# Neighbours' taps of the convolution on ScalarE, and part of the weights' remainders by ScalarE and an accumulating transfer

## The chip, the cores and the metric

The kernel runs on one core of one Trainium2 chip. The metric is the device time of one execution in microseconds, the median of the runs shown. TensorE (PE) does the matrix products, VectorE (DVE), ScalarE (ACT) and GpSimd (POOL) work on tiles in SBUF and PSUM, and SyncE (SP) issues the loads.

## The reference

Two layers of an encoder on 256 tokens of width 2048, all in float32. Each layer normalises its input, projects it, runs two attention groups, projects back, and then does a gated feed-forward with a width-3 convolution over the positions. The change touches the feed-forward:

```python
def depthwise_conv(u, w, bias):
    up = jnp.pad(u, ((0, 0), (1, 1), (0, 0)))
    return up[:, :-2] * w[0] + up[:, 1:-1] * w[1] + up[:, 2:] * w[2] + bias
...
    for l in range(DEPTH):
...
        x = x + o @ w_out[l]
        h2 = rms_norm(x, ln2_g[l])
        u = depthwise_conv(h2 @ w_up[l], conv_w[l], conv_b[l])
        gate, up = u[..., :D_FF], u[..., D_FF:]
        x = x + (jax.nn.silu(gate) * up) @ w_down[l]
```

`w_up` is 2048 x 11264 and `w_down` 5632 x 2048 in each layer.

## The kernel before

**Products in parts.** A float32 product is made of products of fp32r operands. Each operand is split (`split`, lines 109 to 117) into a high part, which ACT rounds (L112), and a remainder, which DVE subtracts (L113). The tile names are `whi` and `wlo` for weights; an activation keeps both parts in one tile (`xs` for the normalised input, `mid` for the gated middle).

**Weights by the megabyte.** All weights come in quanta of 128 x 2048 float32 (1 MB), in the fixed order of the list `quanta`. SP loads each into one of three `raw` buffers (L741); the load of quantum q + 3 is issued when the last piece of quantum q has been split. A quantum is used in two half blocks of 128 x 1024 (three pieces for the seven products). The list `steps` holds these half blocks. `split_w(s + 4)` makes `whi` and `wlo` of the step that lies four ahead, then the step s itself is issued. There are five buffers of each, so a buffer is written again once PE has done with the step that used it five before.

**The up projection.** The 44 feature blocks f of a layer take two quanta each, u = 0 and 1, so four half blocks. In each half block PE does eight pairs (`two`): the high weights by both parts of `xs`, 512 wide, and the remainder of the weights by the high part of `xs`, 256 wide. The sums stand in a PSUM tile `mm`. After the fourth half block `glu(l, f)` follows: ACT copies the sum (L545), DVE adds the second half and scales by the norm into a `halo` tile (L546, L547), POOL copies its two edges (L549, L550), ACT does the centre tap with the bias (L555), DVE adds the four neighbour taps (two neighbours, gate and up; L557), ACT does SiLU (L559), DVE multiplies (L561), and the product is split into `mid`. Every second f forms four sums and differences for the seven products (`sums_mid`, L574 to L577).

**The down projection.** The 44 f of a layer are taken in chunks of 8, 8, 8, 8 and 12. After the ups of a chunk and one more f comes `q_plain` (a plain product of 128 rows, whose sum DVE adds to `x` at L654) and then four `q_seven`: two-by-two blocks by seven products, whose sums stand in PSUM tiles `mm`, `S`, `tr` and `pv`. Between the sevens lie quanta of `w_down` in the 8-wide chunks, and ups in the 12-wide one. The three pieces of a seven quantum need sums of weights, which DVE makes in place in `raw` before the second piece (`split_seven`, L747 to L749); the third piece is made of these too.

**Order.** A scheduler puts the instructions on the engines by their place in the program and by priority; the work of `split_w` has a priority of 40 (`AHEAD_PRIO`) ahead of its place. Each engine then runs its own list in order. Nothing in the scheduler is touched by the change. DMA loads go out on SP's queue; POOL issues none.

**The start.** The loop over `SPLIT_AHEAD` at line 836 makes the first four half blocks, each behind `first_x(i)`, which splits two blocks of `xs` (L115, L116). The first of them is split in two halves of 512 columns.

Of the kernel before, what the change touches and what calls it, by code (L numbers as in the profile page):

```python
# [11 lines left out]
F32 = mybir.dt.float32  # L12
# [6 lines left out]
P = 128  # L19
L = 2  # L20
T = 256
# [38 lines left out]
def encoder_kernel(  # L60
# [343 lines left out]

    quanta = []
    side = {}

    def at(q, f, *args, half=1):
        side.setdefault((q, half), []).append((f, args))

    def two(ps, w_h, w_l, mv, first, last):

        mm(ps, w_h, mv, first, False)
        mm(ps[:, 1], w_l, mv[:, 0], False, last)

# [111 lines left out]
    def q_up(l, f, u):  # L527
        def body(q, half, hi, lo):
            if u == 0 and half == 0:
                cur["up"] = psum.tile([P, 2, 2, T], F32, name="mm", bufs=2)  # L530
            ps = cur["up"]
            hv, lv = (w.rearrange("p (k j n) -> p k j n", k=4, j=2) for w in (hi, lo))
            for j in range(2):
                for kk in range(4):
                    k = 8 * u + 4 * half + kk
                    two(ps[:, j], hv[:, kk, j], lv[:, kk, j], xs[k], k == 0, k == KD - 1)
            if u == 1 and half == 1:
                glu(l, f, ps)
        return body

    def glu(l, f, ps):
# [8 lines left out]
        nc.gpsimd.tensor_copy(ux[:, :, T + r:T + 2 * r - 1], ux[:, :, r + 1:2 * r])  # L550
        y = work.tile([P, 2, T], F32, name="pT", bufs=4)
        for j in range(2):
            c = j * NF + f
            w0, w1, w2, b = (par["conv"][:, l, i, c:c + 1] for i in range(4))
            nc.scalar.activation(y[:, j, :], ux[:, j, r:r + T], AF.Identity, scale=w1, bias=b)  # L555
            for w, o in ((w0, 0), (w2, 2 * r)):
                nc.vector.scalar_tensor_tensor(y[:, j, :], ux[:, j, o:o + T], w, y[:, j, :],  # L557
                                               op0=ALU.mult, op1=ALU.add)
        nc.scalar.activation(t[:, 0, :], y[:, 0, :], AF.Silu)  # L559
# [139 lines left out]
    for l in range(L):  # L699
# [8 lines left out]
        for c, nf in enumerate(CHUNKS):  # L708
            up = lambda f: [(a["w_up"][l, f, u], q_up(l, f, u), "up") for u in range(2)]
            down = lambda nb, g: [(a["w_down"][l, sum(CHUNKS[:c]) // FG + g, nb], q_down(l, c, nb, g), "")]  # L710
# [7 lines left out]
            if nf == PART:  # L718
                for i in range(PAIRS):
                    quanta += seven(i) + down(2 + i // 2, i % 2)  # L720
            else:

                for i in range(PAIRS):
                    quanta += seven(i)
                    if f < NF:
                        quanta += up(f)
                        f += 1
                for nb, g in ((2, 0), (2, 1), (2, 2), (0, 2), (3, 0), (1, 2), (3, 1), (3, 2)):
                    quanta += down(nb, g)


    steps = [(q, h) for q in range(len(quanta)) for h in range(3 if quanta[q][2] == "seven" else 2)]
    raw, hl, left, loads, highs = {}, {}, {}, {}, {}

    def load(q, parts=1):
# [15 lines left out]

    def split_w(s, parts=1):
        if s < len(steps):
# [5 lines left out]
            with tc.high_priority(offset=AHEAD_PRIO if s >= KD // 2 else 0):  # L759
                if kind == "seven":  # L760
                    highs[s] = split_seven(raw[q].rearrange("p (k n) -> p k n", k=4), half, *hl[s])
                else:
                    m = 1024 // parts
                    for j in range(parts):
                        highs[s] = split(*(t[:, j * m:(j + 1) * m] for t in hl[s]),
                                         raw[q][:, half * 1024 + j * m:half * 1024 + (j + 1) * m])
            left[q] -= 1
# [68 lines left out]
    for i in range(SPLIT_AHEAD):  # L836
        first_x(i)
        split_w(i, 2 if i == 0 else 1)
    for n, shape, dt, src in (
# [121 lines left out]
```

## Time and profile before

| what | value |
|---|---|
| median of three runs | 2092.12 us (2092.11 to 2092.13) |
| the profiled execution, its own time | 2092.0 us |
| its span in the trace | 2090.2 us |
| granted TensorE clock | 1.000 |
| ACT busy | 1222.3 us (58%) |
| POOL busy | 170.3 us (8%) |
| moved | 408.42 MB, mean 195 GB/s |
| loads on SP's queue (q1) | 405.46 MB, 56.2% of the 16 DMA engines' span |

The profile is of one execution. Its span runs from the first to the last recorded instruction; 1.8 us of its own time lie outside. An engine's share is its busy time over the span, an average over stages with different limits. In a list of instructions the columns are start, length (both us), engine, line, operation, output and inputs, shape and count, and in brackets what ended the idle time before. A matmul's recorded length is not its spacing from the next: they are pipelined.

### The profile page before, as it was taken

The numbers are of one execution on the slowest core, as the hardware profiler recorded it, in microseconds if no ns is written. First come the engines' busy times: TensorE is split into PE (matmuls) and PEld (weight loads), VectorE is DVE, ScalarE is ACT, GpSimd is POOL, SyncE is SP. The second block draws the span as 40 slices with busy tenths as digits, with TensorE's granted clock in tenths as the row PEclk, the third lists the DMA queues.
The fourth block names the chain that finished last, engine by engine and source line by source line (L and its number), as shares of the span: only waits on it lengthen the run. The fifth ranks groups of instructions, "written<-read, shape, count | busy, mean of one in ns | idle before, by whom it ended". The sixth has DMA issues, their size and how long they took to land.

```text
span 2090.2 us, 29185 instructions
## 1 busy us (share of the span) xinstructions
PE 2083.5 (100%) x10816; PEld 1789.2 (86%) x10816; DVE 1720.5 (82%) x2604; ACT 1222.3 (58%) x1817; POOL 170.3 (8%) x237
## 2 busy tenths in 40 slices
PE   9999999999999999999999999999999999999999
PEld 8888888888888888888888888888888888888887
DVE  7786757898898988989757866678989989899896
ACT  7566556555555556556555665565556555555563
POOL 0011100100101001010000011001001010010100
PEclk9999999999999999999999999999999999999999
DMA  9544555556565564655655444555555655556554
GB/s 350 199 145 164 179 172 174 198 195 211 180 241 182 208 210 167 242 193 211 208 181 181 162 160 166 177 182 189 214 202 170 236 199 204 201 185 234 185 200 161
DMA packets 62144, 408.42 MB, mean 195 GB/s; under 512 B 7344, under 2 KB 9904, under 8 KB 13744
## 3 DMA queue, kind: packets, MB, share of 16 engines
q1 hardware_dynamic: 61280, 405.46, 56.2%
q8 instruction: 85, 1.39, 0.3%
q10 hardware_dynamic: 720, 1.08, 0.2%
q14 instruction: 59, 0.48, 0.1%
HBM read 404.42 MB, written 2.10 MB: 194 GB/s over the span
## 4 chain that ended last, share of the span: by engine, by line
PE 99%; DMA 0%; ACT 0%; DVE 0%; issue 0%
PE mm L98 90%; PE S L98 4%; PE pv L98 3%; PE tr L98 2%; PE tr L373 1%; PE tr L307 1%; PE S L149 1%; DMA head<-in_head 0%; ACT qtok L274 0%; ACT kT L315 0%; ACT xs L115 0%; DVE x L688 0%; ACT whi L112 0%
## 5 line engine op out<-in xcount | busy, mean ns | idle before, releaser
L112 ACT ACTIVATE whi<-raw 128x1024 fp32r<-128x1024 f32 (+1 forms) x797 | 830.9, 1057 | 689.9 <-PE mm L98 411.9
L113 DVE TENSOR_TENSOR wlo<-raw,whi 128x1024 fp32r<-128x1024 f32 (+1 forms) x797 | 963.9, 1220 | 270.3 <-ACT whi L112 231.8
L98 PE MATMUL mm<-xs,whi 128*128 128x512 f32 x2816 | 977.0, 390 | 0.0
L98 PE MATMUL mm<-xs,wlo 128*128 128x256 f32 x2816 | 794.1, 282 | 0.0
L98 PEld LDWEIGHTS mm<-xs,whi 128*128 128x128 f32 x2816 | 528.3, 188 | 110.5
L98 PEld LDWEIGHTS mm<-xs,wlo 128*128 128x128 f32 x2816 | 532.2, 189 | 1.1
L98 PE MATMUL mm<-whi,mid 128*128 128x512 f32 x1412 | 368.2, 391 | 0.0
L98 PEld LDWEIGHTS mm<-whi,mid 128*128 128x128 f32 x1412 | 263.0, 188 | 53.9
L98 PE MATMUL mm<-whi,xs 128*128 128x512 f32 x1152 | 294.2, 393 | 1.4 <-ACT qtok L274 1.3
L98 PEld LDWEIGHTS mm<-whi,xs 128*128 128x128 f32 x1152 | 213.1, 188 | 44.7 <-ACT qtok L274 1.8
L98 PE MATMUL mm<-wlo,mid 128*128 128x512 f32 x706 | 202.4, 392 | 0.0
L98 PE MATMUL mm<-wlo,xs 128*128 128x512 f32 x576 | 159.5, 393 | 0.0
L98 PEld LDWEIGHTS mm<-wlo,mid 128*128 128x128 f32 x706 | 132.1, 188 | 27.0
L557 DVE SCALAR_TENSOR_TENSOR pT<-halo,conv,pT 128x256 f32<-128x256 f32 x352 | 148.1, 478 | 0.9
L549 POOL COPY halo<-halo 128x6 f32<-128x6 f32 x88 | 39.6, 450 | 1232.6 <-DVE halo L547 1232.6
L98 PEld LDWEIGHTS mm<-wlo,xs 128*128 128x128 f32 x576 | 107.3, 188 | 21.6
L555 ACT ACTIVATE pT<-halo,conv 128x256 f32<-128x256 f32 x176 | 95.1, 587 | 5.8 <-DVE halo L547 5.7
L550 POOL COPY halo<-halo 128x6 f32<-128x6 f32 x88 | 77.1, 876 | 0.2 <-POOL halo L549 0.2
L547 DVE TENSOR_TENSOR halo<-prob,acc_b 128x512 f32<-128x512 f32 x88 | 60.6, 689 | 1.9
L546 DVE TENSOR_TENSOR prob<-prob,mm 128x512 f32<-128x512 f32 x88 | 59.8, 679 | 0.0
L545 ACT ACTIVATE prob<-mm 128x512 f32<-128x512 f32 x88 | 51.3, 583 | 7.1 <-PE mm L98 7.1
L559 ACT ACTIVATE prob<-pT 128x256 f32<-128x256 f32 x88 | 35.5, 404 | 30.0 <-DVE pT L557 30.0
(180 smaller groups left out, 1475.4 us busy)
## 6 DMA issues: line engine op xcount, KB each, us to landing
raw<-in_w_up SPq DMA_DIRECT2D x176, 1024.0 KB, 4.9
raw<-in_w_in SPq DMA_DIRECT2D x71, 1024.0 KB, 4.9
raw<-in_w_down SPq DMA_DIRECT2D x48, 1024.0 KB, 4.8
raw<-in_w_seven SPq DMA_DIRECT2D x40, 1024.0 KB, 4.9
raw<-in_w_out SPq DMA_DIRECT2D x32, 1024.0 KB, 4.9
raw<-in_w_plain SPq DMA_DIRECT2D x10, 1024.0 KB, 4.8
bias<-in_bias SPq DMA_DIRECT2D x16, 160.0 KB, 3.1
x<-in_x SPq DMA_DIRECT2D x4, 512.0 KB, 10.7
```

Of the source, the lines that this page charges most:

```text
L98: nc.tensor.matmul(ps, lhsT, rhs, start=start, stop=stop, skip_group_check=True)
L112: high = nc.scalar.activation(hi, src, AF.Copy)
L113: nc.vector.tensor_sub(lo, src, hi.bitcast(F32))
L149: nc.tensor.transpose(ps[:, j, tt * P:(tt + 1) * P], x[:, tt, (k + j) * P:(k + j + 1) * P], ident)
L545: nc.scalar.activation(t, ps[:, :, 0], AF.Copy)
L546: nc.vector.tensor_add(t, t, ps[:, :, 1])
L547: nc.vector.tensor_mul(ux[:, :, r:r + T], t, st["r2"][:, None, :].to_broadcast([P, 2, T]))
L549: nc.gpsimd.tensor_copy(ux[:, :, 1:r], ux[:, :, T:T + r - 1])
L550: nc.gpsimd.tensor_copy(ux[:, :, T + r:T + 2 * r - 1], ux[:, :, r + 1:2 * r])
L555: nc.scalar.activation(y[:, j, :], ux[:, j, r:r + T], AF.Identity, scale=w1, bias=b)
L557: nc.vector.scalar_tensor_tensor(y[:, j, :], ux[:, j, o:o + T], w, y[:, j, :], op0=ALU.mult, op1=ALU.add)
L559: nc.scalar.activation(t[:, 0, :], y[:, 0, :], AF.Silu)
```

## The change

It has four parts.

- **Taps.** In `glu`, the two taps of each neighbour (gate and up) are made by two ACT copies with a scale from the table into a tile `z`, and one DVE addition over both halves adds `z` to `y`. Before, DVE did the four taps by four multiply-add instructions. `y` and `z` share the four buffers of the name `pT`.
- **Remainders.** In the last half block of an f (u = 1, half = 1), unless one of the five steps before it belongs to a seven (`added`), DVE no longer subtracts the remainder. ACT writes the negated weights, rounded to fp32r, into `wlo`; POOL issues a transfer that adds the weights in DRAM to what stands in `wlo`; and ACT makes `whi` as before. The built program holds 82 of these half blocks, of 88 f.
- **Grouping.** In the last half block of every f, `two` takes all eight terms: first the eight products of the high weights, then the eight of the remainders. Elsewhere it goes pair by pair as before.
- **Start.** The first half block's high part is made by DVE, both halves before the first two blocks of `xs`, and its remainder behind them. `split_w` no longer takes a number of parts.

The order of the quanta, of SP's loads, and the number of buffers stay. The lists of `seven` and `down` quanta are appended one by one, so that `up` sees the length of `quanta`.

```diff
@@ -403,15 +403,19 @@
 
 
     quanta = []
+    second = set()
     side = {}
 
     def at(q, f, *args, half=1):
         side.setdefault((q, half), []).append((f, args))
 
-    def two(ps, w_h, w_l, mv, first, last):
-
-        mm(ps, w_h, mv, first, False)
-        mm(ps[:, 1], w_l, mv[:, 0], False, last)
+    def two(terms, late=False):
+
+        for group in [terms] if late else [[t] for t in terms]:
+            for ps, w_h, w_l, mv, first, last in group:
+                mm(ps, w_h, mv, first, False)
+            for ps, w_h, w_l, mv, first, last in group:
+                mm(ps[:, 1], w_l, mv[:, 0], False, last)
 
     def three(ps, terms, hv, lv, first, last, apart=False):
 
@@ -530,10 +534,8 @@
                 cur["up"] = psum.tile([P, 2, 2, T], F32, name="mm", bufs=2)
             ps = cur["up"]
             hv, lv = (w.rearrange("p (k j n) -> p k j n", k=4, j=2) for w in (hi, lo))
-            for j in range(2):
-                for kk in range(4):
-                    k = 8 * u + 4 * half + kk
-                    two(ps[:, j], hv[:, kk, j], lv[:, kk, j], xs[k], k == 0, k == KD - 1)
+            two([(ps[:, j], hv[:, kk, j], lv[:, kk, j], xs[k], k == 0, k == KD - 1)
+                 for j in range(2) for kk, k in enumerate(range(8 * u + 4 * half, 8 * u + 4 * half + 4))], u == half == 1)
             if u == 1 and half == 1:
                 glu(l, f, ps)
         return body
@@ -549,13 +551,15 @@
         nc.gpsimd.tensor_copy(ux[:, :, 1:r], ux[:, :, T:T + r - 1])
         nc.gpsimd.tensor_copy(ux[:, :, T + r:T + 2 * r - 1], ux[:, :, r + 1:2 * r])
         y = work.tile([P, 2, T], F32, name="pT", bufs=4)
+        w = [[par["conv"][:, l, i, j * NF + f:j * NF + f + 1] for i in range(4)] for j in range(2)]
         for j in range(2):
-            c = j * NF + f
-            w0, w1, w2, b = (par["conv"][:, l, i, c:c + 1] for i in range(4))
-            nc.scalar.activation(y[:, j, :], ux[:, j, r:r + T], AF.Identity, scale=w1, bias=b)
-            for w, o in ((w0, 0), (w2, 2 * r)):
-                nc.vector.scalar_tensor_tensor(y[:, j, :], ux[:, j, o:o + T], w, y[:, j, :],
-                                               op0=ALU.mult, op1=ALU.add)
+            nc.scalar.activation(y[:, j, :], ux[:, j, r:r + T], AF.Identity, scale=w[j][1], bias=w[j][3])
+
+        for i, o in ((0, 0), (2, 2 * r)):
+            z = work.tile([P, 2, T], F32, name="pT", bufs=4)
+            for j in range(2):
+                nc.scalar.activation(z[:, j, :], ux[:, j, o:o + T], AF.Copy, scale=w[j][i])
+            nc.vector.tensor_add(y, y, z)
         nc.scalar.activation(t[:, 0, :], y[:, 0, :], AF.Silu)
         m = work.tile([P, T], F32, name="bias", bufs=2)
         nc.vector.tensor_mul(m, t[:, 0, :], y[:, 1, :])
@@ -706,7 +710,10 @@
                     quanta.append((a["w_out"][l, 0 if grp == "a" else 1, nb, u], q_wout(l, grp, nb, u), ""))
         f = 0
         for c, nf in enumerate(CHUNKS):
-            up = lambda f: [(a["w_up"][l, f, u], q_up(l, f, u), "up") for u in range(2)]
+            def up(f):
+                second.add(len(quanta) + 1)
+                return [(a["w_up"][l, f, u], q_up(l, f, u), "up") for u in range(2)]
+
             down = lambda nb, g: [(a["w_down"][l, sum(CHUNKS[:c]) // FG + g, nb], q_down(l, c, nb, g), "")]
             seven = lambda i: [(a["w_seven"][l, c, i], q_seven(l, c, i), "seven")]
 
@@ -717,7 +724,8 @@
             quanta.append((a["w_plain"][l, c], q_plain(l, c), ""))
             if nf == PART:
                 for i in range(PAIRS):
-                    quanta += seven(i) + down(2 + i // 2, i % 2)
+                    quanta += seven(i)
+                    quanta += down(2 + i // 2, i % 2)
             else:
 
                 for i in range(PAIRS):
@@ -732,6 +740,12 @@
     steps = [(q, h) for q in range(len(quanta)) for h in range(3 if quanta[q][2] == "seven" else 2)]
     raw, hl, left, loads, highs = {}, {}, {}, {}, {}
 
+    def added(s):
+
+        q, half = steps[s]
+        return quanta[q][2] == "up" and quanta[q - 1][2] == "up" and half == 1 and q in second and \
+            not any(quanta[steps[i][0]][2] == "seven" for i in range(s - SPLIT_AHEAD - 1, s))
+
     def load(q, parts=1):
         if q < len(quanta):
             raw[q] = wp.tile([P, 2048], F32, name="raw", bufs=3)
@@ -749,7 +763,7 @@
             nc.vector.tensor_sub(w[:, 0], w[:, 3], w[:, 0])
         return split(hv, lv, (w[:, 1::2], w[:, 1:3], w[:, 0::3])[part])
 
-    def split_w(s, parts=1):
+    def split_w(s):
         if s < len(steps):
             q, half = steps[s]
             kind = quanta[q][2]
@@ -760,10 +774,24 @@
                 if kind == "seven":
                     highs[s] = split_seven(raw[q].rearrange("p (k n) -> p k n", k=4), half, *hl[s])
                 else:
-                    m = 1024 // parts
-                    for j in range(parts):
-                        highs[s] = split(*(t[:, j * m:(j + 1) * m] for t in hl[s]),
-                                         raw[q][:, half * 1024 + j * m:half * 1024 + (j + 1) * m])
+                    w = raw[q][:, half * 1024:(half + 1) * 1024]
+                    if s == 0:
+
+                        m = [slice(j * 512, (j + 1) * 512) for j in range(2)]
+                        for j in m:
+                            highs[s] = nc.vector.tensor_copy(hl[s][0][:, j], w[:, j])
+                        first_x(0)
+                        with tc.issue_after(highs[s].ins):
+                            for j in m:
+                                nc.vector.tensor_sub(hl[s][1][:, j], w[:, j], hl[s][0][:, j].bitcast(F32))
+                    elif added(s):
+
+                        nc.scalar.activation(hl[s][1], w, AF.Copy, scale=-1.0)
+                        nc.gpsimd.dma_start(out=hl[s][1], in_=quanta[q][0][:, half * 1024:(half + 1) * 1024],
+                                            accum_op=ALU.add)
+                        highs[s] = nc.scalar.activation(hl[s][0], w, AF.Copy)
+                    else:
+                        highs[s] = split(*hl[s], w)
             left[q] -= 1
             if left[q] == 0:
                 del raw[q]
@@ -834,8 +862,9 @@
         mm(ps[:, 0:P], ones, ones, True, True)
 
     for i in range(SPLIT_AHEAD):
-        first_x(i)
-        split_w(i, 2 if i == 0 else 1)
+        if i > 0:
+            first_x(i)
+        split_w(i)
     for n, shape, dt, src in (
             ("pos", [P, TT], I32, a["pos"]),
             ("inv", [P, HD // 2], F32, a["inv"].partition_broadcast(P))):
```

The rows below show how the issue order of three engines changes. They have the line, the operation, the output and the inputs, and the shape; "x2" stands for two such in a row. Lines after the change are those of the changed kernel (L545, L555, L557, L559, L654 and L747 to L749 become L547, L556, L561 with L562, L563, L658 and L761 to L763).

First ACT's list in one f of an up projection, from the copy of the sum (`prob<-mm`) to the split of the product (`mid<-bias`), before:

```order
L112 ACTIVATE whi<-raw 128x1024
L545 ACTIVATE prob<-mm 128x512
L112 ACTIVATE whi<-raw 128x1024
L555 ACTIVATE pT<-halo_110,conv 128x256 x2
L112 ACTIVATE whi<-raw 128x1024
L559 ACTIVATE prob<-pT 128x256
L112 ACTIVATE whi<-raw 128x1024
L112 ACTIVATE mid<-bias 128x256
```

The same stretch of ACT's list after the change:

```order
L547 ACTIVATE prob<-mm 128x512
L112 ACTIVATE whi<-raw 128x1024
L556 ACTIVATE pT<-halo_112,conv 128x256 x2
L561 ACTIVATE pT<-halo_112,conv 128x256 x4
L112 ACTIVATE whi<-raw 128x1024
L563 ACTIVATE prob<-pT 128x256
L792 ACTIVATE whi<-raw 128x1024
L789 ACTIVATE wlo<-raw 128x1024
L112 ACTIVATE mid<-bias 128x256
```

Four taps stand behind the centre taps (L556), and in one of the four half blocks the negated copy (L789) stands behind the high part (L792).

On POOL the transfer (L790) stands behind the two copies of the halo's edges (L551, L552) of the f before; before the change POOL's list had only the copies there.

Next DVE's list where the ups of an 8-wide chunk end and its sevens begin: from the sum of the plain product (`x<-x,mm`) to the last preparation of the second seven's weights (`raw<-raw`; `mid<-tq,mid` is the remainder of a sum made by `sums_mid`), before:

```order
L654 TENSOR_TENSOR x<-x,mm 128x512
L113 TENSOR_TENSOR wlo<-raw,whi 128x1024
L113 TENSOR_TENSOR mid<-tq,mid 128x256
L113 TENSOR_TENSOR wlo<-raw,whi 128x1024
L557 SCALAR_TENSOR_TENSOR pT<-halo_110,conv,pT 128x256 x2
L113 TENSOR_TENSOR wlo<-raw,whi 128x1024
L557 SCALAR_TENSOR_TENSOR pT<-halo_110,conv,pT 128x256 x2
L747 TENSOR_TENSOR raw<-raw 128x1024
L561 TENSOR_TENSOR bias<-prob,pT 128x256
L748 TENSOR_TENSOR raw<-raw 128x512
L749 TENSOR_TENSOR raw<-raw 128x512
```

The same place of DVE's list after the change:

```order
L658 TENSOR_TENSOR x<-x,mm 128x512
L549 TENSOR_TENSOR halo_110<-prob,acc_b 128x2x256
L113 TENSOR_TENSOR wlo<-raw,whi 128x1024 x2
L113 TENSOR_TENSOR mid<-tq,mid 128x256
L113 TENSOR_TENSOR wlo<-raw,whi 128x1024 x2
L562 TENSOR_TENSOR pT<-pT 128x512
L761 TENSOR_TENSOR raw<-raw 128x1024
L562 TENSOR_TENSOR pT<-pT 128x512
L762 TENSOR_TENSOR raw<-raw 128x512
L113 TENSOR_TENSOR wlo<-raw,whi 128x1024
L763 TENSOR_TENSOR raw<-raw 128x512
```

The sum of the plain product now stands ahead of the halo's product (L549), which stood ahead of it before, and a remainder of weights stands between the second and the third preparation.

Last PE's list at the same place, up to the third piece of the second seven (the two `pv<-whi,mid` at the end; `mm`, `tr`, `S` and `pv` are the PSUM tiles of the sums), before:

```order
L98 MATMUL mm<-whi,mid 128x512 x8
L98 MATMUL mm<-wlo,mid 128x512 x4
L98 MATMUL mm<-whi,mid 128x512 x8
L98 MATMUL tr<-whi,mid 128x512 x2
L98 MATMUL mm<-whi,mid 128x512 x2
L98 MATMUL mm<-wlo,mid 128x512 x4
L98 MATMUL tr<-wlo,mid 128x512
L98 MATMUL mm<-wlo,mid 128x512
L98 MATMUL S<-whi,mid 128x512 x4
L98 MATMUL pv<-whi,mid 128x512 x2
```

PE's list there after the change:

```order
L98 MATMUL pv<-wlo,mid 128x512
L98 MATMUL mm<-wlo,mid 128x512
L98 MATMUL tr<-whi,mid 128x512 x2
L98 MATMUL mm<-whi,mid 128x512 x2
L98 MATMUL mm<-wlo,mid 128x512 x4
L98 MATMUL mm<-whi,mid 128x512 x8
L98 MATMUL mm<-wlo,mid 128x512 x4
L98 MATMUL tr<-wlo,mid 128x512
L98 MATMUL mm<-wlo,mid 128x512
L98 MATMUL S<-whi,mid 128x512 x4
L98 MATMUL S<-wlo,mid 128x512 x2
L98 MATMUL pv<-whi,mid 128x512 x2
```

Two remainder products (`S<-wlo,mid`) now stand ahead of the third piece's first product: 51 products lie between the plain product's last one and that, 49 before.

## The prediction

> **What bounds the kernel now.** I read the page's head and its chain first, then busy time by stretch, then groups of instructions, then the timeline where the lead of the helpers is smallest.
>
> ```profile
> span 2090.2 us, 29185 instructions
> ...
> PE 2083.5 (100%) x10816; PEld 1789.2 (86%) x10816; DVE 1720.5 (82%) x2604; ACT 1222.3 (58%) x1817; POOL 170.3 (8%) x237
> ...
> PE 99%; DMA 0%; ACT 0%; DVE 0%; issue 0%
> ...
> 597.40:692.10 94.70, 94.70 (x540) 83.59 (x539) 83.02 (x128) 54.79 (x79) 8.39 (x14) 1.00 0.59 204
> 692.10:727.00 34.90, 34.90 (x155) 28.90 (x155) 34.59 (x40) 21.11 (x25) 1.18 (x2) 1.00 0.56 202
> ```
>
> The last two rows are a stretch of up projections and the stretch of seven-product down projections behind it (columns: PE, PEld, DVE, ACT, POOL, clock, DMA share and GB/s). The chain is PE for 99%, and PE has no gap in either stretch, at the full granted clock. DVE is at 88% in the ups (83.02 of 94.70) and at 99% in the sevens. So work taken from DVE in the ups can gain nothing by itself: PE does not wait for it. The question is only whether PE starts to wait somewhere. It can do so where the split weights arrive latest before their use, and that is early in each seven stretch. DVE and ACT enter it some 10 us ahead and use that lead up:
>
> ```profile
> 692.84 0.62 PE L98 MATMUL mm<-wlo,mid 128*128 128x512 f32 x2
> ...
> 704.40 0.62 PE L98 MATMUL pv<-whi,mid 128*128 128x512 f32 x2
> ...
> 703.05 3.91 ACT L112 ACTIVATE whi<-raw 128x1024 fp32r<-128x1024 f32 x4 [0.32 <-DVE raw L749]
> ...
> 692.39 0.68 DVE L547 TENSOR_TENSOR halo<-prob,acc_b 128x512 f32<-128x512 f32 x1
> ...
> 694.13 0.68 DVE L654 TENSOR_TENSOR x<-x,mm 128x512 f32<-128x512 f32 x1
> 694.73 1.22 DVE L113 TENSOR_TENSOR wlo<-raw,whi 128x1024 fp32r<-128x1024 f32 x1
> 695.86 0.42 DVE L113 TENSOR_TENSOR mid<-tq,mid 128x256 fp32r<-128x256 f32 x1
> ...
> 697.33 0.87 DVE L557 SCALAR_TENSOR_TENSOR pT<-halo,conv,pT 128x256 f32<-128x256 f32 x2
> ...
> 700.05 1.22 DVE L747 TENSOR_TENSOR raw<-raw 128x1024 f32<-128x1024 f32 x1
> 701.19 0.42 DVE L561 TENSOR_TENSOR bias<-prob,pT 128x256 f32<-128x256 f32 x1
> 701.53 0.68 DVE L748 TENSOR_TENSOR raw<-raw 128x512 f32<-128x512 f32 x1
> 702.24 0.69 DVE L749 TENSOR_TENSOR raw<-raw 128x512 f32<-128x512 f32 x1
> 702.85 1.22 DVE L113 TENSOR_TENSOR wlo<-raw,whi 128x1024 fp32r<-128x1024 f32 x1
> ```
>
> Columns: start, length, engine, line, tiles, count. The first PE row is the end of the plain product. The second uses the high part of the third piece of the second seven. ACT makes that piece as the first of the four at 703.05, when DVE's L749 ends (702.93): done at 703.05 + 1.06 = 704.11, used at 704.40. **The lead there is 0.3 us.** The other stretches between 8-wide chunks look the same, eight in all.
>
> **What the change removes and adds.**
>
> ```profile
> L112 ACT ACTIVATE whi<-raw 128x1024 fp32r<-128x1024 f32 (+1 forms) x797 | 830.9, 1057 | 689.9 <-PE mm L98 411.9
> ...
> L113 DVE TENSOR_TENSOR wlo<-raw,whi 128x1024 fp32r<-128x1024 f32 (+1 forms) x797 | 963.9, 1220 | 270.3 <-ACT whi L112 231.8
> ...
> L557 DVE SCALAR_TENSOR_TENSOR pT<-halo,conv,pT 128x256 f32<-128x256 f32 x352 | 148.1, 478 | 0.9
> ...
> L115 ACT ACTIVATE xs<-S,head 128x256 fp32r<-128x256 f32 x48 | 20.7, 469 | 12.0 <-PE S L149 8.8 <-DVE xs L116 3.2
> ```
>
> Taps: 352 DVE instructions of 478 ns go; 176 additions of 0.68 us (as L547 above) and 352 ACT instructions come, each near the 469 ns of L115, the nearest ACT row with one scale from a table. DVE gains 168 - 120 = 48 us, ACT gets 165. Remainders: the built program has 82 of them. DVE loses 82 x 1.22 = 100 us, ACT gets 82 x 1.06 = 87. All of it lies beside PE. In an up stretch of eight f, DVE falls to about 83.02 - 8 x 1.2 - 8 x 0.5 = 69 us of 94.70, and ACT rises to 54.79 + 8 x (1.0 + 4 x 0.47) = 78. Both keep up.
>
> The Trainium skill (ScalarE: Activation LUTs, Rules for kernel authors) says to put multiplications and additions on VectorE, not ScalarE. By it the taps would get dearer. The rows do not bear it out for these fp32 tiles (478 against 469 ns), so the sum stays as it is.
>
> Does ACT fit in detail? One f of an up stretch now:
>
> ```profile
> 400.39 1.06 ACT L112 ACTIVATE whi<-raw 128x1024 fp32r<-128x1024 f32 x1 [1.24 <-PE mm L98]
> 401.36 1.08 ACT L555 ACTIVATE pT<-halo,conv 128x256 f32<-128x256 f32 x2
> 403.15 1.06 ACT L112 ACTIVATE whi<-raw 128x1024 fp32r<-128x1024 f32 x1 [0.72 <-ACT pT L555]
> 405.93 1.06 ACT L112 ACTIVATE whi<-raw 128x1024 fp32r<-128x1024 f32 x1 [1.42 <-PE mm L98]
> 408.70 1.06 ACT L112 ACTIVATE whi<-raw 128x1024 fp32r<-128x1024 f32 x1 [0.78 <-ACT mid L112]
> ...
> 401.50 1.26 POOL L550 COPY halo<-halo 128x6 f32<-128x6 f32 x1
> ```
>
> PE frees a buffer every 2.77 us (405.93 to 408.70). After L555 ends at 402.44 come four taps, the last two not before POOL's copy ends (402.76): until about 404.5. The high part of 403.15 slips to 404.5, that of 405.93 stays, SiLU takes 0.4, and the negated copy runs 407.3 to 408.4, just before the buffer of 408.70. ACT fits.
>
> **The transfer.** PE takes up a block four half blocks after its buffer came free: 405.9 + 4 x 2.77 = 417.0. Eight wide products (0.227 us each, below) come first, so the remainder is wanted at 418.8, and 10.4 us remain after the copy. No row shows an accumulating transfer. Nearest are these:
>
> ```profile
> raw<-in_w_up SPq DMA_DIRECT2D x176, 1024.0 KB, 4.9
> ...
> x<-in_x SPq DMA_DIRECT2D x4, 512.0 KB, 10.7
> ```
>
> 4.9 us for twice the bytes, and 10.7 us for the same bytes in the crowded first 30 us. I take 5 to 9, near the first, because the ups leave the DMA engines 41% idle: no cost. At 10.7 it would be 0.3 us late 82 times, 25 us. Each further microsecond costs 82 us. Behind the waiting matmuls stands all of PE; behind the transfer on POOL stand only the next f's halo copies.
>
> The Trainium skill (DMA: Bandwidth & Descriptors, Anatomy of one DMA) gives 2.0 us plus bytes over 436 GB/s for a transfer issued by POOL, 3.2 us here as an estimate, and says nothing there of the addition. By it the transfer is hidden with 7 us to spare, as by the 4.9 us row.
>
> **Grouping.** In the last half block of an f eight 512-wide products now precede eight 256-wide ones.
>
> ```profile
> 399.55 0.39 PE L98 MATMUL mm<-xs,whi 128*128 128x512 f32 x1
> ...
> 399.90 0.39 PE L98 MATMUL mm<-xs,whi 128*128 128x512 f32 x1
> ...
> L98 PE MATMUL mm<-xs,wlo 128*128 128x256 f32 x2816 | 794.1, 282 | 0.0
> ...
> 172.07 0.85 PE L98 MATMUL pv<-pT,v_b 128*128 128x256 f32 x6
> ...
> 7.11 1.90 ACT L115 ACTIVATE xs<-mid,head 128x256 fp32r<-128x256 f32 x4
> 8.91 1.05 ACT L112 ACTIVATE whi<-raw 128x1024 fp32r<-128x1024 f32 x1
> ...
> 10.01 2.11 PE L98 MATMUL mm<-whi,xs 128*128 128x512 f32 x8
> ...
> 15.59 1.98 PE L98 MATMUL mm<-whi,xs 128*128 128x512 f32 x8
> ```
>
> An alternating pair takes 0.35 us. In runs of its own kind a 512 takes 0.227 (the last plain product starts at 692.84 + 0.62 - 0.39 = 693.07, and 50 products lie from there to 704.40) and a 256 takes (0.85 - 0.28) / 5 = 0.114 (six in 0.85, one lasts 0.28), 0.341 in all. The gain is 0 to 5 ns for each of 704 pairs; I take 1 ns, **-0.7 us**.
>
> **The start.** DVE now makes the first high part. But PE runs without gaps only from 10.01, when ACT has the next high part (8.91 + 1.05). Before it ACT makes four xs whose last source lands late. Bounds: 0, or the 1.0 us that ACT is spared. I take **-0.2**, near nothing.
>
> **The second seven, where I see the loss.** The issue order of DVE changes at that place. Before: sum of the plain product (L654), remainder, mid, remainder, two taps, remainder, two taps, L747, L561, L748, L749. After: sum, halo, two remainders, mid, two remainders, addition, first preparation, addition, second preparation, **a remainder, and only then the third preparation**. The order cannot start before the plain product is in: 693.07 + 0.39 = 693.46 (first PE row), so 693.55; before, DVE came to it late anyway, at 694.13. From there, start to start by the rows above: sum 0.60, halo 0.60, four remainders 4 x 1.13, mid 0.34, additions 2 x 0.60, preparations 1.14 and 0.60, and a remainder 1.14 with 0.1 of waiting for ACT. That is 10.2 us, so the third preparation starts at 703.8 and ends 0.69 later at 704.5. ACT follows 0.12 later (702.93 to 703.05) and takes 1.06: **705.65**. PE's own order puts two more products ahead of the piece, so it wants it at 704.40 + 2 x 0.227 = 704.85. It waits 0.8 us, 0.05 for the hand-over and 0.13 to get going (eight products take 2.11 us behind the wait that ends at 10.01, 1.98 at 15.59): **1.0 us, eight times, 8.0 us**. In the two wide chunks the same sum and halo come ahead of two remainders, with the second wanted 16 products (3.6 us) after the plain product: ready at 0.26 + 0.6 + 0.6 + 1.13 + 1.22 = 3.8, late by 0.2 and 0.15 for hand-over and start: 0.7 us for both.
>
> Sum against the profiled execution (2092.0 us, span 2090.2 and 1.8 around it; the median of the runs is 2092.12): 2092.0 + 8.0 + 0.7 - 0.7 - 0.2 = **2099.8 us**.
>
> **Rivals.** (1) *PE does not wait: no change.* It decides at one number: if the DVE chain from the plain product to the third piece is 0.85 us shorter than my 12.1, PE arrives as late as the piece. For it: the chain is a sum of a dozen durations, and DVE is relieved just before. Against it: the chain is tied to PE's plain product, which relief does not move. Then 2092.0 - 0.9 = 2091.1, or 2092 without the small gains. (2) *The transfer comes late*, past 10.4 us: 2092 + 82 us for each microsecond, so 2117 at 10.7. For it: the addition has to read the old content too, and POOL can be held up:
>
> ```profile
> L549 POOL COPY halo<-halo 128x6 f32<-128x6 f32 x88 | 39.6, 450 | 1232.6 <-DVE halo L547 1232.6
> L550 POOL COPY halo<-halo 128x6 f32<-128x6 f32 x88 | 77.1, 876 | 0.2 <-POOL halo L549 0.2
> ```
>
> The same small copy takes 450 or 876 ns, and 1.26 where a DVE remainder runs beside it. One such hold-up costs the transfer 1.2 us of its 10.4. The Trainium skill (SBUF — State Buffer, Who interferes with whom) has DVE instructions with two SBUF inputs block only a GpSimd instruction that reads SBUF, and not the writing of descriptors. These copies agree; no run here shows the descriptors. (3) *A gain above 0.2%* (4.2 us, about what a measurement of this kernel can tell from no change) would need grouping at its bound and the start at its bound, 3.5 + 1.0, and no wait.
>
> **How the numbers follow.** Forecast 0.54, own range 2096 to 2106 (a chain 0.5 us shorter or 0.8 longer, ten places). Rival 1: 0.31. Rival 2: 0.12. Rival 3: 0.03. To leave out no more than 2 in 10 the range runs from 2091.0 to 2107. Slower: 0.54 x 0.95 + 0.12 = 0.63. Same: 0.34. Faster: 0.03.
>
> **What would show it.** Right: gaps of PE only at the third piece of the second seven, about 1 us, named as waits for ACT's whi, with DVE's L658 at the plain product's end and the third preparation (L763) behind a remainder; none in the ups. Rival 1: those gaps are missing. Rival 2: PE waits for a transfer to wlo in the ups, once per f. Wrong altogether: PE products that change their spacing, or a late load of raw, since the transfers add 43 MB to 408.

## The result and the profile after

The changed kernel takes 2106.34 us (median of 4 runs, 2103.49 to 2107.76), the kernel before 2092.12 us. The ratio is 1.0066, with a 95% interval of 1.005 to 1.0082: **slower by 14 us**. The profiled execution took 2105.57 us, 13.6 more than that of before.

The page of the changed kernel: head, chain, two groups (busy us and mean ns of one behind the bar) and two rows of the DMA issues (KB each, median us to landing):

```profile
span 2103.5 us, 29426 instructions
...
PE 2089.9 (99%) x10816; PEld 1784.8 (85%) x10816; DVE 1606.5 (76%) x2348; ACT 1424.2 (68%) x2249; POOL 211.4 (10%) x319
...
PE 96%; DMA 1%; DVE 1%; ACT 1%; issue 0%; ACTq 0%; DVEq 0%
...
L562 DVE TENSOR_TENSOR pT<-pT 128x512 f32<-128x512 f32 x176 | 121.6, 691 | 53.2 <-ACT pT L561 44.7
...
L561 ACT ACTIVATE pT<-halo,conv 128x256 f32<-128x256 f32 x352 | 149.5, 496 | 1.6 <-POOL halo L551 0.2
...
raw<-in_w_up SPq DMA_DIRECT2D x176, 1024.0 KB, 5.7
...
wlo<-in_w_up POOLq DMA_DIRECT2D x82, 512.0 KB, 7.8
```

DVE's busy time fell by 114 us, ACT's rose by 202, and the chain shows that PE, which was 99% of it, now waits. What for is in the view of waits of PE (us in total, times, longest):

```profile
PE pv L98 <- ACT whi L112: 4.8, 8, 0.6
...
PE mm L98 <- DMA wlo<-in_w_up: 1.2, 2, 0.8
```

Eight waits for the high part of a third piece, and two for a transfer. The stretch of ups and the seven stretch behind it, in the columns of the prediction's windows:

```profile
599.00:695.50 96.50, 96.50 (x547) 84.63 (x546) 73.50 (x105) 73.29 (x116) 12.14 (x22) 1.00 0.85 251
695.50:732.00 36.50, 35.90 (x159) 29.30 (x158) 35.07 (x40) 23.26 (x29) 2.25 (x2) 1.00 0.51 189
```

In the ups the work moved as intended (DVE 83 to 74 us, ACT 55 to 73), and PE has no gap in this one. In the sevens DVE is nearly as full as before, and PE has a gap. One of the eight waits, from the timelines of DVE, ACT and PE (start, length, engine; in brackets the idle time before and what ended it):

```profile
697.41 0.69 DVE L658 TENSOR_TENSOR x<-x,mm 128x512 f32<-128x512 f32 x1 [0.33 <-PE mm L98]
698.01 0.69 DVE L549 TENSOR_TENSOR halo<-prob,acc_b 128x512 f32<-128x512 f32 x1
698.62 2.35 DVE L113 TENSOR_TENSOR wlo<-raw,whi 128x1024 fp32r<-128x1024 f32 x2
...
705.84 0.69 DVE L762 TENSOR_TENSOR raw<-raw 128x512 f32<-128x512 f32 x1
706.50 1.23 DVE L113 TENSOR_TENSOR wlo<-raw,whi 128x1024 fp32r<-128x1024 f32 x1
707.64 0.68 DVE L763 TENSOR_TENSOR raw<-raw 128x512 f32<-128x512 f32 x1
...
708.42 2.01 ACT L112 ACTIVATE whi<-raw 128x1024 fp32r<-128x1024 f32 x2 [1.65 <-DVE raw L763]
...
708.32 0.61 PE L98 MATMUL S<-wlo,mid 128*128 128x512 f32 x2
709.53 0.73 PE L98 MATMUL pv<-whi,mid 128*128 128x512 f32 x2 [0.60 <-ACT whi L112]
```

DVE waits for PE's plain product (0.33 idle), and the third preparation starts 707.64 - 697.41 = 10.23 us behind its sum. ACT follows, and PE starts the piece at 709.53 instead of 708.32 + 2 x 0.227 = 708.77: 0.76 us late, with 0.11 more over the next two products (0.73 against 0.62).

### The profile page after: what moved, and what is told of

It reads as the page before. It is cut to its first block, busy times and chain, and to the rows that moved or that the text cites. A ratio compares the mean times of both kernels' runs of the same rounds, so it can differ in the third digit from the quotient of the medians.

```text
span 2103.5 us, 29426 instructions
## 1 busy us (share of the span) xinstructions
PE 2089.9 (99%) x10816; PEld 1784.8 (85%) x10816; DVE 1606.5 (76%) x2348; ACT 1424.2 (68%) x2249; POOL 211.4 (10%) x319
## 4 chain that ended last, share of the span: by engine, by line
PE 96%; DMA 1%; DVE 1%; ACT 1%; issue 0%; ACTq 0%; DVEq 0%
PE mm L98 87%; PE S L98 3%; PE pv L98 3%; PE tr L98 1%; DMA wlo<-in_w_up 1%; PE tr L373 1%; PE tr L307 1%; PE S L149 0%; ACT whi L112 0%; DVE wlo L113 0%; DMA mid<-in_xT 0%; DVE raw L763 0%; DVE pT L562 0%; ACT qtok L274 0%; DVE halo L549 0%
## 5 line engine op out<-in xcount | busy, mean ns | idle before, releaser
L113 DVE TENSOR_TENSOR wlo<-raw,whi 128x1024 fp32r<-128x1024 f32 x713 | 861.9, 1222 | 299.9 <-ACT whi L112 242.2
L112 ACT ACTIVATE whi<-raw 128x1024 fp32r<-128x1024 f32 x713 | 739.8, 1054 | 475.9 <-PE mm L98 297.3
L98 PE MATMUL mm<-xs,whi 128*128 128x512 f32 x2816 | 910.4, 392 | 0.0
L98 PE MATMUL mm<-xs,wlo 128*128 128x256 f32 x2816 | 691.0, 281 | 1.2 <-DMA wlo<-in_w_up 1.2
L98 PEld LDWEIGHTS mm<-xs,wlo 128*128 128x128 f32 x2816 | 492.5, 189 | 11.5 <-DMA wlo<-in_w_up 2.0
L562 DVE TENSOR_TENSOR pT<-pT 128x512 f32<-128x512 f32 x176 | 121.6, 691 | 53.2 <-ACT pT L561 44.7
L790 POOL DMA_DIRECT2D wlo<-in_w_up x82 | 71.6, 874 | 824.3 <-ACT wlo L789 674.5
L561 ACT ACTIVATE pT<-halo,conv 128x256 f32<-128x256 f32 x352 | 149.5, 496 | 1.6 <-POOL halo L551 0.2
L792 ACT ACTIVATE whi<-raw 128x1024 fp32r<-128x1024 f32 x82 | 86.6, 1056 | 43.0 <-PE mm L98 41.2
L556 ACT ACTIVATE pT<-halo,conv 128x256 f32<-128x256 f32 x176 | 95.5, 589 | 2.6 <-DVE halo L549 2.6
L551 POOL COPY halo<-halo 128x6 f32<-128x6 f32 x88 | 47.5, 539 | 454.9 <-DVE halo L549 454.9
L789 ACT ACTIVATE wlo<-raw 128x1024 fp32r<-128x1024 f32 x82 | 85.6, 1043 | 0.0
L549 DVE TENSOR_TENSOR halo<-prob,acc_b 128x512 f32<-128x512 f32 x88 | 60.6, 688 | 4.5
```

The lines of the kernel that those rows point to most:

```text
L98: nc.tensor.matmul(ps, lhsT, rhs, start=start, stop=stop, skip_group_check=True)
L112: high = nc.scalar.activation(hi, src, AF.Copy)
L113: nc.vector.tensor_sub(lo, src, hi.bitcast(F32))
L549: nc.vector.tensor_mul(ux[:, :, r:r + T], t, st["r2"][:, None, :].to_broadcast([P, 2, T]))
L551: nc.gpsimd.tensor_copy(ux[:, :, 1:r], ux[:, :, T:T + r - 1])
L561: nc.scalar.activation(z[:, j, :], ux[:, j, o:o + T], AF.Copy, scale=w[j][i])
```

## The experiments

Each was timed beside the kernel before: 2092.08 us with e1 to e4, 2092.16 with e5 to e8, 2092.17 with e9 to e12.

| kernel | median us (lowest to highest) | ratio, 95% interval |
|---|---|---|
| e1 changed, remainder behind third preparation | 2106.11 (2105.88 to 2107.37) | 1.0068 (1.0056 to 1.0081) |
| e2 taps alone | 2101.07 (2100.89 to 2101.19) | 1.0043 (1.003 to 1.0055) |
| e3 grouping alone | 2094.85 (2094.69 to 2095.07) | 1.0013 (1.0004 to 1.0022) |
| e4 remainders alone | 2100.17 (2098.56 to 2100.83) | 1.0036 (1.0024 to 1.0049) |
| e5 e1, tap additions later too | 2129.82 (2129.33 to 2132.82) | 1.0182 (1.0169 to 1.0196) |
| e6 start alone | 2092.43 (2092.29 to 2092.76) | 1.0001 (0.9993 to 1.001) |
| e7 remainders and grouping | 2095.49 (2095.0 to 2096.58) | 1.0016 (1.0007 to 1.0025) |
| e8 e3, halves in turn | 2094.89 (2094.73 to 2095.2) | 1.0013 (1.0004 to 1.0022) |
| e9 changed, ten f without tap additions | 2096.34 (2095.92 to 2097.82) | 1.0021 (1.0012 to 1.003) |
| e10 e5, a sum later | 2101.54 (2100.82 to 2105.58) | 1.0049 (1.0037 to 1.0062) |
| e11 changed, fewer transfers | 2103.45 (2103.1 to 2105.13) | 1.0055 (1.0042 to 1.0068) |
| e12 e10 and e11 | 2100.61 (2100.24 to 2104.15) | 1.0044 (1.003 to 1.0058) |

### The parts alone: e2, e3, e4, e6

**e2** is the kernel before with the new `glu` only.

> The kernel before, with the taps' part of the change alone. Theory A: the taps by themselves change DVE's order where the sevens begin, so the eight waits at the third piece of the second seven are there: 2092.1 + 7.0 = 2099.1 (2097 to 2101). Rival B: the waits need the remainders' part too (another load on ACT); then no gap and 2092 within 0.5.

Measured: +9.0 us. The taps alone give DVE the order of the changed kernel at the second seven, and PE's starts fall behind those of before by 0.91 to 0.96 us at each of the eight places (7.5 in all), by 0.38 at the first ups of the two wide chunks, by 0.3 at the start, and nowhere else. Its view of waits of PE has the same line as the changed kernel's:

```profile
PE pv L98 <- ACT whi L112: 4.8, 8, 0.6
```

Theory A holds: relieving DVE in the ups brings the loss, since the scheduler's order at the sevens changes with it.

**e3** is the kernel before with the new `two` and its call.

> The kernel before, with the grouping alone (remainders still by DVE). Theory A: in groups of their own kind the 512-wide products of the ups are started 233 ns apart and the 256-wide 117, against 228 and 118 in alternation; with two slower ones behind each group some 38 ns a block, times 88: 2092.1 + 3.3 = 2095.4 (2094.5 to 2096.5). Rival B: the wider spacing is caused by the accumulating transfers' traffic or by the taps on ACT; then spacings are 228 and 118, and the time is 2092.1 or up to 1 us under it.

Measured: +2.8 us, with no transfer and no new tap in the kernel. The timeline of PE around one group of e3:

```profile
417.17 2.02 PE L98 MATMUL mm<-xs,whi 128*128 128x512 f32 x8
419.03 1.09 PE L98 MATMUL mm<-xs,wlo 128*128 128x256 f32 x8
419.97 0.40 PE L98 MATMUL mm<-xs,whi 128*128 128x512 f32 x1
...
420.32 0.39 PE L98 MATMUL mm<-xs,whi 128*128 128x512 f32 x1
...
422.40 0.39 PE L98 MATMUL mm<-xs,whi 128*128 128x512 f32 x1
```

Eight 512-wide products take 419.03 - 417.17 = 1.86 us (0.2325 each), eight 256-wide 0.94 (0.1175): 2.80. In alternation behind it six pairs take 2.08, so eight take 2.77. That is 0.03 us a group, 88 x 0.03 = 2.6. Rival B falls.

**e4** is the kernel before with `added`, used pair by pair.

> The kernel before, with the remainders' part alone: negated copy by ACT and accumulating transfer, but the remainder's products used pair by pair. Theory A: the transfer needs 8.0 to 9.5 us from the copy's end, mostly 8.1, and PE now wants it 1.6 us earlier than with the grouping, about 9 us behind the copy: some 15 to 25 of 82 blocks are late, by 0.1 to 2.5 us each: 2098 to 2112, with a spread between runs of several us. Rival B: the transfers are never late by themselves, and the few waits in the changed kernel come from the taps that ACT does ahead of the copy: then 2092.1 to 2094.

Measured: +8.1 us, spread 2.3 us. The view of the transfer's line of e4 (who waited, us and times; then all 82 transfers):

```profile
  PEld mm L98: 7.6, 10
  PE mm L98: 4.5, 6
...
DMA to landing us min/median/max: 7.6/7.8/11.0
```

PE (its weight loads) waited ten times, not 15 to 25, but the sum and the spread are those of theory A. DVE's taps of before are in this kernel, so the taps on ACT aren't needed for it.

**e6** is the kernel before with DVE's first high part and the later remainder.

> The kernel before, with the start's part alone. Theory A: the dense stretch of PE begins with ACT's second high part, which stands behind four xs; sparing ACT the first high part moves nothing, since the last xs source lands late, and the 0.25 us that PE is behind at the 200th product of the changed kernel come from that landing: 2092.1 within 0.4. Rival B: DVE's remainders ahead of its xs, or ACT's later high part, cost the 0.25 us each time: 2092.35 in every run. Rival C, as predicted: 2091.9.

Measured: 0.27 us more, every run above the median of before. The ACT timeline of e6:

```profile
8.15 0.91 ACT L115 ACTIVATE xs<-mid,head 128x256 fp32r<-128x256 f32 x2 [0.79 <-DMA mid<-in_xT]
8.97 1.04 ACT L112 ACTIVATE whi<-raw 128x1024 fp32r<-128x1024 f32 x1
```

ACT waits for the source of the last `xs`, and the second high part ends where it did (10.01 against 9.96 before). That is theory A's late source, and it gives 0.04 to 0.05 of the 0.27. Rival B's size is met in the median, but the trace doesn't show it at the start: from there PE is 0.04 us behind the trace of before, and 0.12 more comes at the first stretch of sevens. The traces of e2 and e7, kernels without the start's part, are 0.3 and 0.6 us behind at the start, so this place differs by more than that from one execution to the next. What makes every run of e6 longer is not settled; rival C falls.

### The grouping's two sides: e7, e8

**e7** has the remainders and the grouping, with DVE's taps.

> The kernel before, with remainders by copy and transfer and with the grouping, taps by DVE. Theory A: the grouping gives the transfer 1.6 us more, so that only the blocks close behind the sevens are late, as in the changed kernel: 2092.1 + 2.8 (grouping, as in e3) + 0 to 2.5 = 2095 to 2097.5. Rival B: lateness does not depend on the grouping: 2092.1 + 2.8 + 8 = 2103. Rival C: without the taps on ACT no transfer is late: 2094.9.

Measured: +3.3 us, 0.6 above e3. In its trace weight loads waited twice for a transfer, 1.0 us in all, both in the first three f behind a stretch of sevens. Theory A holds: the grouping costs 2.8, but it takes 7.5 off what the transfers cost without it (8.1 in e4, 0.6 here).

**e8** changes the order within a group:

```diff
-                 for j in range(2) for kk, k in enumerate(range(8 * u + 4 * half, 8 * u + 4 * half + 4))], u == half == 1)
+                 for kk, k in enumerate(range(8 * u + 4 * half, 8 * u + 4 * half + 4)) for j in range(2)], u == half == 1)
```

> The grouping alone as in e3, but in a group each next product goes to the other half of the sum (gate and up in turn, another PSUM bank each) instead of four to one and four to the other. Theory A: the wider spacing (233 against 228 ns) comes from successive products into one bank: then 228 and 2092.1 or up to 1 us under. Rival B: it comes from the weights that follow each other (stationary whi after whi), whatever the bank: 2094.9 as in e3.

Measured: as e3. That successive products go to one half of the sum isn't the cause (theory A falls). What in the succession of wide products costs 5 ns each is not settled.

### The waits at the second seven: e1, e5, e10, e9

**e1** puts the remainder behind the third preparation, in `split_seven`:

```diff
-            nc.vector.tensor_sub(w[:, 0], w[:, 3], w[:, 0])
+            third = nc.vector.tensor_sub(w[:, 0], w[:, 3], w[:, 0])
+            high = nc.scalar.activation(hv, w[:, 1:3], AF.Copy)
+            with tc.issue_after(third.ins):
+                nc.vector.tensor_sub(lv, w[:, 1:3], hv.bitcast(F32))
+            return high
```

> The changed kernel, with DVE's remainder of a seven's second piece issued behind the third preparation. Theory A: the eight waits of PE at the third piece of the second seven (0.77 us idle and 0.11 to get going each in the changed kernel's trace) come from DVE's order there. Without them the median falls by 8 x 0.88 = 7.0 us, from 2106.3 to about 2099.3 (2097 to 2102), and PE has no gap over 0.1 us at the pv products. Rival B: PE is held there by work that it would meet a little later anyway; then a wait appears within the same seven stretch and the median stays above 2103.

Measured: no gain. Theory A in this form falls; the median lies where rival B put it, for a reason that neither names. The same place in e1, timelines of DVE, POOL, ACT and PE:

```profile
698.37 1.22 DVE L113 TENSOR_TENSOR wlo<-raw,whi 128x1024 fp32r<-128x1024 f32 x1
699.50 0.42 DVE L113 TENSOR_TENSOR mid<-tq,mid 128x256 fp32r<-128x256 f32 x1
699.84 2.36 DVE L113 TENSOR_TENSOR wlo<-raw,whi 128x1024 fp32r<-128x1024 f32 x2
703.22 0.69 DVE L562 TENSOR_TENSOR pT<-pT 128x512 f32<-128x512 f32 x1 [1.02 <-ACT pT L561]
...
698.51 3.73 POOL L551 COPY halo<-halo 128x6 f32<-128x6 f32 x1 [13.23 <-DVE halo L549]
...
702.27 1.71 ACT L561 ACTIVATE pT<-halo,conv 128x256 f32<-128x256 f32 x4 [2.69 <-POOL halo L551]
...
708.18 0.73 PE L98 MATMUL pv<-whi,mid 128*128 128x512 f32 x2 [0.63 <-ACT whi L112]
```

DVE has two remainders less in the chain, but the tap addition ahead of the preparations now waits for ACT's taps, these wait for POOL's halo copy, and the copy lasts until DVE's run of remainders ends (702.2). The third piece is still 0.8 us late, at all eight places. Beside that, two waits of 1.4 us come at the first ups of the wide chunks. One wait took the place of another.

**e5** defers the taps of the ten f ahead of a plain product and adds this:

```diff
+            if late:
+                with tc.issue_after(st["third"].ins):
+                    nc.vector.tensor_add(y, y, z)
```

> The kernel of e1 (remainder of the second piece behind the third preparation), and in the ten f ahead of a plain product DVE's tap additions are issued behind the third preparation as well. Theory A: in e1 the eight waits stayed because the preparations stood behind a tap addition that waited for ACT's taps, which waited for POOL's halo copy (3.73 us instead of 0.19 beside DVE's remainders). With the additions out of the way the third preparation is done over 2 us earlier and the eight waits are gone: 2106.1 - 7.0 = 2099.1 (2097.5 to 2101; the two waits of 1.4 us that e1 has in the wide chunks may stay). Rival B: ACT's high part of the third piece stands behind the taps that wait for POOL, so PE still waits there: above 2103.

Measured: +37.7 us, far above theory A, and not for rival B's reason. The second seven itself runs through, and the next does not (PE, then DVE, then PE):

```profile
712.74 0.62 PE L98 MATMUL pv<-whi,mid 128*128 128x512 f32 x2
...
718.90 0.68 DVE L773 TENSOR_TENSOR raw<-raw 128x512 f32<-128x512 f32 x1
721.10 1.22 DVE L485 TENSOR_TENSOR x<-x,mm 128x1024 f32<-128x1024 f32 x1 [1.51 <-PE mm L98]
722.24 0.68 DVE L774 TENSOR_TENSOR raw<-raw 128x512 f32<-128x512 f32 x1
...
724.15 0.74 PE L98 MATMUL pv<-whi,mid 128*128 128x512 f32 x2 [1.73 <-ACT whi L112]
```

The edit let the scheduler put the sum of a down projection between two preparations of the third seven. That sum waits for PE, and PE then waits for what stands behind it.

**e10** issues that sum behind the third preparation (`add_x` in `q_down`, in the same way).

> The kernel of e5, with the sum of the first down quantum pair (x, L485) issued behind the third preparation of the seven that follows. Theory A: in e5 the second seven no longer waits, and its new waits (1.89 us at the third seven, 1.57 us at the next ups, eight each) come from that sum: it waits for PE and stands ahead of the third seven's third preparation on DVE. Behind it, both are gone: 2129.8 - 8 x 3.4 = 2102, less the knock-on, 2098 to 2102. Rival B: DVE lacks time in the stretch whatever the order, and PE waits elsewhere: above 2104.

Measured: 28 us back, +9.4 over before. PE runs through at the second and the third seven. At the fourth it is held a little (timeline of PE, then the view of its waits):

```profile
724.01 1.07 PE L98 MATMUL S<-whi,mid 128*128 128x512 f32 x4
725.08 0.73 PE L98 MATMUL pv<-whi,mid 128*128 128x512 f32 x2
...
PE mm L98 <- DVE prob L548: 2.5, 2, 1.2
```

The third piece of the fourth seven starts at 725.08 instead of 724.01 + 4 x 0.227 = 724.92. With getting going, each of the eight stretches still sets PE back by 0.29 us, 2.4 in all, so a small part of rival B is there as well. The pair of waits in the wide chunks stands as in e1, and sets PE back by 1.5 us each. The rest is the grouping, one late transfer and the start.

**e9** is the changed kernel without the two tap additions in ten f, so its sums lack the neighbours' taps there:

```diff
-            nc.vector.tensor_add(y, y, z)
+            if f not in (8, 16, 24, 32, 40):
+                nc.vector.tensor_add(y, y, z)
```

> The changed kernel without DVE's two tap additions in the ten f ahead of a plain product (their neighbours' taps are left out of the sum). Theory A: PE's eight waits are DVE's chain from the plain product to the third preparation of the second seven; it becomes shorter by two additions of 0.60 us and a remainder that then stands behind the third preparation, over 2 us, so the waits of 0.77 us are gone: 2106.3 - 7.5 = 2098.8 (2097 to 2101). Rival B: DVE lacks time in the whole seven stretch, so a wait comes back at the next seven or at its end, as in e5: above 2103.

Measured: 10.0 us less than the changed kernel. Timelines of DVE, ACT and PE of e9 at the same place:

```profile
703.06 0.69 DVE L764 TENSOR_TENSOR raw<-raw 128x512 f32<-128x512 f32 x1
...
703.84 3.91 ACT L112 ACTIVATE whi<-raw 128x1024 fp32r<-128x1024 f32 x4 [0.60 <-DVE raw L764]
...
704.45 1.07 PE L98 MATMUL S<-whi,mid 128*128 128x512 f32 x4
705.36 0.62 PE L98 MATMUL pv<-whi,mid 128*128 128x512 f32 x2
```

The high part is ready at 703.84 + 1.06 = 704.9, wanted at 705.36: no wait, at any of the eight places, and the only new hold of PE elsewhere is one of 0.5 us in the last wide chunk. With 1.2 us of additions less and a remainder later, DVE has time enough for the whole stretch. That it gained 10.0, not 7.5, goes with the transfers: in this trace they made weight loads wait once, for 0.5 us. Why fewer are late here was not tried.

### The late transfers: e11, e12

In the changed kernel the worst transfer (11.4 us to landing) is issued in the second f behind a seven stretch. PE's timeline there:

```profile
492.47 2.02 PE L98 MATMUL mm<-xs,whi 128*128 128x512 f32 x8
495.24 0.97 PE L98 MATMUL mm<-xs,wlo 128*128 128x256 f32 x6 [0.75 <-DMA wlo<-in_w_up]
```

Just before, SP's loads follow each other by 2.3 to 5.5 us (issued at 466.5, 468.8, 471.6, 474.6 and 480.1, against some 5.6 apart later), and from 475 to 486 the DMA engines are busy all the time (share 1.00, against 0.79 from 497 to 508).

**e11** is the changed kernel with none in the first two f behind the sevens (66 transfers):

```diff
-            not any(quanta[steps[i][0]][2] == "seven" for i in range(s - SPLIT_AHEAD - 1, s))
+            not any(quanta[steps[i][0]][2] == "seven" for i in range(s - SPLIT_AHEAD - 9, s))
```

> The changed kernel without transfers in the first two f behind each seven stretch that had them (DVE makes those remainders). Theory A: the late transfers are those issued while loads of 1 MB that were held back in the sevens are caught up (10.2 and 11.4 us to landing there, 7.8 elsewhere); without them PE waits for no transfer, the eight waits at the sevens stay: 2104 (2103 to 2105), and the runs lie within 0.6 us of each other instead of 4.3. Rival B: transfers are late anywhere now and then: the spread stays over 2 us and the median about 2106.

Measured: 2.9 us less than the changed kernel. The view of the transfer's line names no waiter any more, and:

```profile
DMA to landing us min/median/max: 7.6/7.8/9.1
```

Four of five runs lie within 0.5 us of each other; the fifth is 1.5 above. Theory A holds for the place and the size, but not for all of the spread. The other traces agree on the place: in all kernels with transfers, each one that took 10 us or more was wanted in the first four f behind a stretch of sevens.

**e12** joins e10 and e11.

> The kernels of e10 and e11 in one: DVE's order mended, no transfers close behind the sevens. Theory A: what is left is grouping 2.8, start 0.3 and the wide chunks' waits (0.8, or 2.8 with the reordered remainder as in e1): 2092.1 + 3.9 to 5.9 = 2096 to 2098, runs within 0.6 us. Rival B: the ups' relief of DVE comes back as a gain somewhere: under 2094.

Measured: +8.4 us, 2.6 above the expected range, with four runs within 0.5 us and one 3.4 above them. Nothing comes back as a gain (rival B falls). What theory A left out is in the trace: the third piece of the fourth seven sets PE back by 0.29 us in each of the eight stretches, as in e10. With 2.4 for these, 3.0 for the two waits in the wide chunks, 2.8 for the grouping and 0.3 at the start the sum is 8.5. The runs that stand out have no trace, so their cause stays open.

No kernel here is faster than the one before.

## Why the prediction was right

**The whole.** The direction and the largest loss came as worked out, at the place named. But the measured 2106.34 us lies 0.3 above the forecast's own range (2096 to 2106) and inside only the wider one (to 2107), and about 6 of the 14 us came from terms forecast as gains or at nothing. That the total still fell in the range is in part luck. Of the signs set down for being right, "none in the ups" failed: PE waited for a transfer there, which was the sign of rival 2, though at 2 of 82 and not once per f. And products changed their spacing, a sign set down for being wrong altogether. The loads of `raw` took longer (5.7 us against 4.9 for `w_up`), but PE's waits name none.

**The second seven** (8.0 us forecast, 7.5 measured in e2's trace, 7.4 in the changed kernel's). Every link was as worked out: DVE tied to the plain product, the third preparation 10.2 us behind it (10.23), ACT behind that, PE late by 0.8 (0.76). e2 shows that the taps bring the order and e9 that the chain decides. Not foreseen was that the chain has a second strand, from POOL's copy over ACT's taps to DVE's addition, only just shorter, as e1 showed.

**The wide chunks** (0.7 forecast, 0.76 in e2, 0.57 in the changed kernel). Right.

**Grouping** (-0.7 forecast, +2.8 in e3). This step failed, and in sign. The 0.227 us for a 512-wide product came from rows in which the weights stream past stationary `mid`. In the ups the weights are the stationary side, and such products one behind another are 0.2325 apart. The 0.114 of a 256-wide product, from an attention row, was 0.1175. Rows of the same shape in another role set the bound.

**The start** (-0.2 forecast, +0.27 in e6's median). A late source holds ACT up, as the step said, so nothing is gained. What costs the 0.27 is not shown.

**The transfer** (nothing forecast, 0.6 in e7, 2.9 at e11's places). This step failed too. The 5 to 9 us taken holds for the median, 7.8, and the room of about 10.4 for nearly all. The tail was missing: 11.4 us where loads held back in the sevens are caught up. The price of 82 us for each microsecond would hold only if all 82 were late alike. The Trainium skill's formula (DMA: Bandwidth & Descriptors, Anatomy of one DMA) gave 3.2 us as an estimate; measured are 7.6 to 11.4, and the measurement decides.

**Taps and remainders.** An ACT tap takes 496 ns, where 469 was taken, and hides beside PE as forecast. DVE's relief was put at 48 + 100 = 148 us and is 114. The sum added up lengths of instructions that overlap: the row of the old taps has 148.1 us busy, not 352 x 0.478 = 168.

The sum from the runs: 7.5 + 0.8 + 2.8 + 0.3 + 2.9 = 14.3 us, against 14.2 between the medians. That they agree so well is chance in part, since the runs of the changed kernel spread over 4.3 us. In its profiled execution PE's last product is 13.1 us later than before: 7.4 at the second sevens, 0.6 at the wide chunks, 0.2 at the start, 1.8 at the two late transfers, and 3.1 spread over the rest, where the grouping is. The forecast of 7.7 was short by the grouping's 3.5, the transfers' 2.9 and the start's 0.5, and over by 0.4 at the sevens.

## What to carry to other kernels

Where one engine is busy throughout, relief of another gains nothing and can still cost: a scheduler reorders what it finds early, and an in-order engine then holds a piece behind work that isn't urgent. Look for the place with the smallest lead, and write out the chain to it in the new order. Price a product by rows with the same operand in the same role, and a transfer by its slowest place, not by its median.

## What was not expected

A halo copy of POOL and its issues of the transfer in the changed kernel (one undisturbed copy and the two at the second seven from the timeline; all issues from the view of their line, ns min/median/max):

```profile
423.39 0.19 POOL L551 COPY halo<-halo 128x6 f32<-128x6 f32 x1 [2.69 <-DVE halo L549]
...
698.76 1.12 POOL L551 COPY halo<-halo 128x6 f32<-128x6 f32 x1 [12.52 <-DVE halo L549]
699.82 1.20 POOL L552 COPY halo<-halo 128x6 f32<-128x6 f32 x1
...
L790 POOL DMA_DIRECT2D wlo<-in_w_up x82: 862/865/1063, 328.9 to 1991.3; - x82
```

The same copy took 3.73 us in e1, until a run of DVE remainders and a `mid` ended. The Trainium skill (SBUF — State Buffer, Who interferes with whom) has a DVE instruction with two SBUF inputs contend with a GpSimd instruction that reads SBUF. The trace agrees (0.19 against 3.73). In e1 the copy did not get in between DVE instructions that follow each other closely, at any of the eight places. In the changed kernel it did: at the place shown each copy ended with one of two remainders in a row (1.12 and 1.20). What decides this is not shown. The issues took 0.86 to 1.06 us each, so none was held up in this way.

The order of two instructions on DVE, at eight places, cost 28 us (e5 against e10), twice what the whole change did.
